# Seven-product groups combined in PSUM banks, and from group 1 on in the first FFN

## The chip, the cores and the metric

One core of a Trainium2 chip runs the whole program. Its engines work beside one another and each runs its own instructions in order: TensorE (PE; its weight loads are listed as PEld), VectorE (DVE), ScalarE (ACT), GpSimd (POOL) and SyncE (SP), which here does nothing but issue transfers. They meet at semaphores. The metric is the device time of one execution in microseconds; the median of three runs of the kernel before is 918.29 us.

## The reference

Two layers of an encoder over 256 tokens of width 1024, all float32. Each layer adds half of a SwiGLU FFN, then attention, then half of a second FFN; a last norm closes the trunk. The change concerns the four FFNs:

```python
def swiglu(h, w_gate, w_up, w_down):
    return (jax.nn.silu(h @ w_gate) * (h @ w_up)) @ w_down
...
    for l in range(DEPTH):
        x = x + 0.5 * swiglu(rms_norm(x, ffn1_norm[l]), ffn1_w_gate[l], ffn1_w_up[l], ffn1_w_down[l])
        ...
        x = x + 0.5 * swiglu(rms_norm(x, ffn2_norm[l]), ffn2_w_gate[l], ffn2_w_up[l], ffn2_w_down[l])
```

The gate and up matrices are 1024 x 2816, the down matrix is 2816 x 1024. The attention between them (windowed heads with a sink, and differential heads) is left as it is but for the PSUM banks that it uses.

## The kernel before

**Float32 by three products.** Every weight is split into a high part, which ScalarE casts, and a low part, which VectorE gets by subtracting it; activations are split alike. A product is three matmuls per chunk of 128 rows: high times high, low times high, high times low. Weights come as raw tiles of 512 rows by 512 columns (1 MB, six buffers, `N_RAW`), loaded by SP (line 153); each is split in two halves of 128x1024 into a pool of 28 tiles (`emit_split`, line 191).

**Order.** `specs` lists the weight steps in the order of use. `weights()` (line 249) takes the next one, and first lets `ahead()` (line 228) issue loads up to 10 steps ahead and splits up to `look` half steps ahead. So the place of every cast and subtraction in ScalarE's and VectorE's queues is fixed by where `weights()` is called and by `look`. All instructions are recorded by one helper (line 50), so the profile gives them the line L50; one has to go by tiles: `raw` is a loaded weight, `w` its parts, `s` activations and hidden values, `q` and `v` sums of activations, `ps` a bank, `tmp` an intermediate.

**One FFN.** The 2816 hidden columns are five groups of 512 (0 to 4) and a rest of 256. The down step of a group, two halves of 24 matmuls of 128x512, is interleaved with the products of the next group, so that TensorE has work while the hidden values are made and transposed.

**Seven products.** Gate and up of a group, for two token blocks and two halves of the 1024 rows, are eight products of 12 matmuls. `by_seven` (line 637) makes them with seven, in the manner of Strassen and Winograd, from sums of the activations (`make_sums`, line 349) and sums of the weights. With a the upper half of the gate matrix, b and c the upper and lower half of the up matrix and d the lower half of the gate matrix, the weights used are a, d, c, a+b, b+c, a+b+c and a+b+c+d. Two sums are made by accumulating DMAs on GpSimd's queue (`gather`, line 126: b into a, c into b), which read memory and add to the raw tile; two by VectorE in the raw tile (`plus`, line 131). `SEVEN` says which groups do so: 2 to 4 in the first FFN, 1 to 4 in the other three. Before, the step b+c stands near the front of the group, so that b is loaded early; the products go to separate banks, are copied out by ScalarE and combined by VectorE in five operations of 128x512.

**PSUM.** All eight banks belong to one rotating tag, `ps`.

**The start of the program.** The first FFN begins while its weights still arrive. GpSimd's queue there holds the norm's rsqrt (`r`), then the constants of the attention (small loads, an iota, a few small operations), then the first accumulating DMAs; these are held back by `issue` and let go by `flush` (lines 165 and 171).

Of the kernel before, what the change touches and what calls it, by code (L numbers as in the profile page):

```python
# [9 lines left out]
F32 = mybir.dt.float32  # L10
F32R = mybir.dt.float32r
AF = mybir.ActivationFunctionType
# [18 lines left out]
SEVEN = ((2, 3, 4), (1, 2, 3, 4))  # L31
# [3 lines left out]
def trunk(ctx: ExitStack, tc: tile.TileContext, x, n1, g1, u1, d1, nm, w_in, sink,  # L35
# [35 lines left out]
    def bank():  # L71
        return ps.tile([P, 512], F32, tag="ps", bufs=8, name=nm_("ps"))
# [19 lines left out]
    class Step:  # L92
        def __init__(self, kn, n, moves, key=None, prep=None, src=None, free=None, behind=None):
            self.kn, self.n, self.moves, self.prep = kn, n, moves, prep
# [20 lines left out]
    def seven(wg, wu, c0, downs, first):  # L115
# [112 lines left out]
    def ahead(n):  # L228

        n = min(n, 2 * len(specs) - 1)  # L230
        while True:
# [4 lines left out]
            elif at["prep"] <= min(n // 2 + 1, len(specs) - 1) and at["dma"] > at["prep"] and \  # L236
                    (specs[at["prep"]].prep is None or at["split"] >= 2 * at["prep"]):
# [21 lines left out]
    for l in range(DEPTH):  # L259
        def ffn_specs(wg, wu, wd, sevens):  # L260
# [45 lines left out]
    class Norm:  # L306
# [42 lines left out]
        def make_sums(self):  # L349
# [19 lines left out]
            s1 = add(b1, t1, ALU.subtract)  # L369
            s2 = add(s1, t0, ALU.add)  # L370
# [159 lines left out]
    def tokens(accs, xs, w, k0, ks=range(4), first=0, last=KC - 1, order=None, cols=slice(None), h=None):  # L530

        for k, t in (order or [(k, t) for k in ks for t in range(2)]):
            kk = k0 + k
            hi, lo = w.part(k, cols, h)
            xv = xs[kk // 2][:, kk % 2]
            xh, xl = xv[:, t * P:(t + 1) * P], xv[:, S + t * P:S + (t + 1) * P]
# [23 lines left out]
    def first_groups(norm, ws):  # L560

        sls = [halves(bank()) for _ in ws]
# [39 lines left out]
    def ffn(norm, aside=None, before=None, final=False, sevens=SEVEN[1]):  # L602
# [34 lines left out]
        def by_seven(h, g):  # L637
# [3 lines left out]

            def put(o, x, y, op):
                dve.tensor_tensor(o, x, y, op=op)
                return o

            late, run = g == max(sevens), 1 in sevens
            m1, m7 = flat(), flat()


            if g > 1:  # L650
                g0 = prod(norm.quarter(0, 0), weights())
                act.copy(m1, g0)
                p7 = prod(norm.summed(3), weights(1, True))
                act.copy(m7, p7)
                hT = turn(h, 2)
                prod(norm.quarter(0, 1), weights(), g0)
                p3 = prod(norm.summed(2), weights())
                if not run:
                    g0 = silu(flat(), g0, 0)
                down(hT, g - 1, 0, weights())  # L660
                if run:
                    g0 = silu(flat(), g0, 0)
            else:
                p1 = prod(norm.quarter(0, 0), weights(1, True))
                hT = turn(h, (0,))
                w = weights(1, True)
                act.copy(m1, p1)
                p2 = prod(norm.quarter(0, 1), w)
                hT += turn(h, (1,))
                g0 = put(flat(), p2, m1, ALU.add)  # L670
                down(hT, 0, 0, weights())
                silu(g0, g0, 0)
                p3 = prod(norm.summed(2), weights())
                p7 = prod(norm.summed(3), weights(1, True))
                act.copy(m7, p7)
            h = blk(F32)
            p5 = prod(norm.summed(0), weights())
            prod(norm.summed(1), weights(look[0] - 5 if late else run, late or run), p7)
            u1 = put(m1, p7, m1, ALU.subtract)
            p4 = prod(norm.quarter(1, 1), weights(look[0] - 4 if late else 3 * run, late or run))  # L680
            g1 = put(flat(), p4, u1, ALU.subtract)
            w = weights(look[0] - 3 if late else 2 * run)
            silu(g1, g1, 1)
            put(u1, u1, p5, ALU.subtract)
            u0 = put(m7, u1, m7, ALU.subtract)
            put(u0, u0, p3, ALU.add)
            if run and g == max(sevens) - 1:
                ahead(2 * at["use"] - 2 + look[0] - 1)
            up(h, u0, g0, 0)
            up(h, u1, g1, 1)  # L690
            down(hT, g - 1, 1, w)
# [14 lines left out]
        accs = [[bank(), bank()] for _ in range(2)]  # L706

        def down(hT, g, h, w):
# [453 lines left out]
```

## Time and profile before

| quantity | value |
| --- | --- |
| runs | 917.40, 918.29, 919.19 us; median 918.29 |
| profiled execution | 917.39 us, its span 915.6 us |
| granted TensorE clock, mean | 0.999 |
| 128x512 matmuls from weights | 2538 by `s`, 540 by `q`, 180 by `v` |
| weight splits of 128x1024 | 354 casts (ACT), 354 subtractions (DVE) |
| raw sums on VectorE, 128x1024 | 60 |
| accumulating DMAs (GpSimd's queue) | 30 of 1 MB |
| loaded by SP's queue, share of 16 DMA engines | 166.74 MB, 54.5% |
| accumulated, share of 16 DMA engines | 31.75 MB, 19.3% |

A group row of the profile names the operation with its tiles, the shapes, the count, then busy time and the mean of one in ns, then the idle time of the engine before it with what ended it. A timeline row gives start and duration in us, the engine, the operation and how many are merged; in brackets the idle time before and what ended it. A row of windows gives for a stretch of time how long each engine was busy, the granted TensorE clock, the share of the DMA engines and the rate. The time from issue to landing of a DMA counts from its instruction to the arrival of its data.

### The profile page before, as it was taken

What the parts mean: (1) busy time and instruction counts of PE and PEld (TensorE: products, weight loads), DVE (VectorE), ACT (ScalarE), POOL (GpSimd) and SP (SyncE); (2) the same over time, 40 slices, a digit from 0 to 9 for tenths busy, and PEclk for the clock granted to TensorE, in tenths of its full rate; (3) what the DMA queues carried; (4) which work ended last, traced back from release to release, by engine and by line L of the source; (5) the groups of instructions that cost most, each with busy time, mean ns of one, the idle gap of its engine ahead of it and who ended that gap; (6) DMA issues with size and microseconds to landing.
All of it is one profiled execution on the core that took longest, in us unless ns stands there. A gap on an engine that the chain in (4) does not pass through costs nothing.

```text
span 915.6 us, 12544 instructions
## 1 busy us (share of the span) xinstructions
PE 904.5 (99%) x4696; PEld 763.7 (83%) x4696; DVE 792.5 (87%) x1096; ACT 589.8 (64%) x917; POOL 66.4 (7%) x83
## 2 busy tenths in 40 slices
PE   8999999999999999999999999999999999999997
PEld 6888888899888888888888888888998888888886
DVE  6768999959975999999789999997797689999994
ACT  7836676557865766576486666665677496666561
POOL 0400100000010100100010010000001010010011
PEclk9999999999999999999999999999999999999999
DMA  9996898828436698898767998887463467998831
GB/s 339 355 238 173 265 297 268 238 93 240 136 108 189 158 280 248 257 273 275 258 164 201 276 285 217 265 293 219 116 230 98 139 153 201 275 289 230 259 132 47
DMA packets 114061, 200.87 MB, mean 219 GB/s; under 512 B 3662, under 2 KB 31376, under 8 KB 114000
## 3 DMA queue, kind: packets, MB, share of 16 engines
q1 hardware_dynamic: 96528, 166.74, 54.5%
q0 software_dynamic: 16096, 31.75, 19.3%
q10 hardware_dynamic: 1376, 1.57, 0.5%
q8 instruction: 37, 0.61, 0.3%
q14 instruction: 24, 0.20, 0.1%
HBM read 199.00 MB, written 1.05 MB: 218 GB/s over the span
## 4 chain that ended last, share of the span: by engine, by line
PE 98%; issue 1%; DMA 0%; ACT 0%; DVE 0%; POOLq 0%; POOL 0%; ACTq 0%
PE ps L50 98%; DMA xk<-in_x_dram 0%; ACT w L50 0%; DVE s L50 0%; DVE xk L50 0%; ACT tmp L50 0%; ACT L50 0%; POOLq L1157 0%; POOL rf L50 0%; ACTq L50 0%; DVE tot L50 0%; DVE tmp L50 0%
## 5 line engine op out<-in xcount | busy, mean ns | idle before, releaser
L50 PE MATMUL ps<-w,s 128*128 128x512 f32 (+1 forms) x2574 | 600.2, 391 | 0.5 <-ACT tmp L50 0.5
L50 PEld LDWEIGHTS ps<-w,s 128*128 128x128 f32 x2574 | 477.6, 188 | 100.3 <-ACT tmp L50 2.3
L50 DVE TENSOR_TENSOR w<-raw,w 128x1024 fp32r<-128x1024 f32 (+1 forms) x458 | 482.1, 1101 | 37.8 <-ACT w L50 36.6
L50 ACT CAST w<-raw 128x1024 fp32r<-128x1024 f32 (+1 forms) x458 | 409.8, 954 | 122.6 <-DVE raw L50 78.4
L50 PE MATMUL ps<-w,q 128*128 128x512 f32 x540 | 127.3, 389 | 0.0
L50 PEld LDWEIGHTS ps<-w,q 128*128 128x128 f32 x540 | 101.4, 188 | 21.0
L50 PE MATMUL ps<-s,w 128*128 128x256 f32 x672 | 83.1, 284 | 0.0
L50 PEld LDWEIGHTS ps<-s,w 128*128 128x128 f32 x672 | 81.5, 192 | 0.5
L50 POOL DMA_DIRECT2D raw<-in_ffn_w_up_dram x30 | 38.9, 1296 | 472.8 <-DVE w L50 240.8
L50 DVE TENSOR_TENSOR raw<-raw,raw 128x1024 f32<-128x1024 f32 x60 | 70.7, 1219 | 0.0
L50 ACT ACTIVATE s<-ps,gcol 128x256 fp32r<-128x256 f32 (+1 forms) x80 | 31.7, 480 | 43.7 <-PE ps L50 42.1
L50 ACT CAST s<-ps 128x512 fp32r<-128x512 f32 x44 | 24.3, 594 | 29.9 <-PE ps L50 29.9
L50 PE MATMUL ps<-w,v 128*128 128x512 f32 x180 | 43.3, 389 | 0.0
L50 ACT COPY tmp<-ps 128x512 f32<-128x512 f32 x34 | 19.9, 585 | 36.2 <-PE ps L50 34.0
L50 ACT ACTIVATE s<-s,negm 128x256 f32<-128x256 f32 x64 | 31.9, 500 | 14.8 <-DVE negm L50 14.8
L50 PE MATMUL ps<-ident,s 128*128 128x128 f32 x304 | 39.7, 273 | 0.0
L50 PEld LDWEIGHTS ps<-w,v 128*128 128x128 f32 x180 | 33.8, 188 | 7.0
L50 PEld LDWEIGHTS ps<-ident,s 128*128 128x128 f32 x304 | 35.1, 140 | 5.1 <-issue 0.8
L50 DVE TENSOR_TENSOR s<-ps,s 128x512 fp32r<-128x512 f32 x44 | 28.7, 686 | 9.1 <-ACT s L50 9.1
L50 DVE SCALAR_TENSOR_TENSOR s<-ps,gcol,s 128x256 fp32r<-128x256 f32 x48 | 20.3, 478 | 11.6 <-ACT s L50 11.5
L50 DVE TENSOR_TENSOR tmp<-ps,tmp 128x512 f32<-128x512 f32 x37 | 25.4, 686 | 2.7 <-PE ps L50 2.1
L50 DVE TENSOR_TENSOR xk<-xk,ps 128x512 f32<-128x512 f32 (+1 forms) x25 | 14.1, 598 | 14.9 <-PE ps L50 14.9
(106 smaller groups left out, 404.7 us busy)
## 6 DMA issues: line engine op xcount, KB each, us to landing
raw<-in_ffn_w_down_dram SPq DMA_DIRECT2D x44, 1024.0 KB, 8.9
raw<-in_ffn_w_gate_dram SPq DMA_DIRECT2D x39, 1024.0 KB, 6.4
raw<-in_ffn_w_up_dram SPq DMA_DIRECT2D x39, 1024.0 KB, 5.7
raw<-in_ffn_w_up_dram POOLq DMA_DIRECT2D x30, 1024.0 KB, 12.3
raw<-in_w_in_dram SPq DMA_DIRECT2D x14, 1024.0 KB, 6.1
raw<-in_ffn_w_gate_dram SPq DMA_DIRECT2D x8, 512.0 KB, 6.2
raw<-in_ffn_w_up_dram SPq DMA_DIRECT2D x8, 512.0 KB, 7.2
raw<-in_w_in_dram SPq DMA_DIRECT2D x8, 512.0 KB, 5.3
```

The source lines that it names most:

```text
L50: ins = issue(*a, **k)
```

## The change

All four FFNs make groups 1 to 4 with seven products. `by_sevens` holds all seven groups of an FFN in one function. ScalarE writes the negated first product into both halves of a two-bank tile (`xy`), and TensorE adds the products of two activation sums on top, one into each half. The product with a+b is copied by ScalarE into the bank of the first one before the product with a+b+c is added to it; the two activation sums involved change sign. VectorE combines the rest in three operations. The two-bank tile takes two of the eight banks and also serves other places: the up products of group 0, the rest, and some banks of the attention.

The second half of a group's down step moves into the next group, after its first product (`below`), and the hidden values are transposed by token (`turn_one`). The weight steps of a group become a, below, d, c, down, a+b, b+c, a+b+c, a+b+c+d, and b is loaded for the step b+c. In group 1 there is no `below` and the order is a, d, down, c. VectorE's sum of two raw tiles is one operation of 128x2048 instead of two of 128x1024, and is issued a step earlier (`early`). `lead` sets `look` per group.

```diff
-SEVEN = ((2, 3, 4), (1, 2, 3, 4))
+SEVEN = ((1, 2, 3, 4), (1, 2, 3, 4))
...
-        return ps.tile([P, 512], F32, tag="ps", bufs=8, name=nm_("ps"))
+        return ps.tile([P, 512], F32, tag="ps", bufs=6, name=nm_("ps"))
+
+    def pair():
+        return ps.tile([P, 2, 512], F32, tag="xy", bufs=1, name=nm_("xy"))
...
-    def seven(wg, wu, c0, downs, first):
+    def seven(wg, wu, c0, below, down):
...
-                for h in (0, 2):
-                    x_, t_ = [raws[i][:, h:h + 2] for i in (x, to)]
-                    dve.tensor_tensor(t_, t_, x_, op=ALU.add)
+                dve.tensor_tensor(raws[to], raws[to], raws[x], op=ALU.add)
             return prep
 
-        bc = Step(4, 512, load(b), key=b, behind=gather(c, b))
-        rest = [Step(4, 512, load(d), key=d, free=[]), Step(4, 512, load(c), key=c, free=[]), downs[0]]
-        steps = [rest[0], rest[2], rest[1], bc] if first else [bc] + rest
+        steps = [Step(4, 512, load(d), key=d, free=[]), Step(4, 512, load(c), key=c, free=[])]
+        steps = [below] + steps + [down] if below is not None else [steps[0], down, steps[1]]
         steps[0].prep = lambda: issue(gather(b, a), 1)
         return [Step(4, 512, load(a), key=a, free=[])] + steps + [
                 Step(4, 512, None, src=a, free=[]),
-                Step(4, 512, None, prep=plus(c, a), src=a, free=[c]),
-                Step(4, 512, None, prep=plus(d, a), src=a, free=[a, d]),
-                downs[1]]
+                Step(4, 512, load(b), key=b, behind=gather(c, b)),
+                Step(4, 512, None, prep=plus(c, a), src=a, free=[c], early=1),
+                Step(4, 512, None, prep=plus(d, a), src=a, free=[a, d])]
 
...
-                    (specs[at["prep"]].prep is None or at["split"] >= 2 * at["prep"]):
+                    (specs[at["prep"]].prep is None or at["split"] >= 2 * (at["prep"] - specs[at["prep"]].early)):
...
-                    specs.extend(seven(wg[l], wu[l], g * 512, downs, g == 1))
+                    specs.extend(seven(wg[l], wu[l], g * 512, down(g - 2, 1) if g > 1 else None, downs[0]))
+                    if g == max(sevens):
+                        specs.append(downs[1])
                 else:
                     specs.extend(plain(w[l], g * 512, 512, k0, 4) for w in (wg, wu) for k0 in (0, 4))
-                    specs.extend(downs)
+                    specs.extend(downs[:1] if g + 1 == min(sevens) else downs)
...
-            s1 = add(b1, t1, ALU.subtract)
-            s2 = add(s1, t0, ALU.add)
+            s1 = add(t1, b1, ALU.subtract)
+            s2 = add(t0, s1, ALU.subtract)
...
-        def by_seven(h, g):
...
+        def turn_one(h, t):
+            sl = bank()
+            for k in range(4):
+                pe.transpose(sl[:, k * P:(k + 1) * P], h[:, t, k * P:(k + 1) * P], ident)
+            hb = blk()
+            act.copy(hb[:, 0], sl)
+            dve.tensor_tensor(hb[:, 1], sl, f(hb[:, 0]), op=ALU.subtract)
+            return hb
+
+        def by_token(hb):
+            return lambda k, t: [hb[t][:, i, k * P:(k + 1) * P] for i in range(2)]
+
+        def by_chunk(hT):
+            return lambda k, t: [hT[k // 2][:, k % 2, i * S + t * P:i * S + (t + 1) * P] for i in range(2)]
+
+        def below(of, g, h, w, order=None):
+            while len(accs) <= h:
+                accs.append([bank(), bank()])
+            tokens(accs[h], of, w, 4 * g, last=(FC - 1, G4 - 1) if final and h else FC - 1, order=order)
+
+        def by_sevens(h, groups, old):
+            xy = pair()
+            for g in groups:
+                start, late = old is None, g == groups[-1]
+                look[0] = lead(g)
+                p1 = prod(norm.quarter(0, 0), weights(start, start))
+                act.activation(xy, p1.unsqueeze(1).to_broadcast([P, 2, 512]), AF.Copy, scale=-1.0)
+                if start:
+                    g0 = flat()
+                    act.copy(g0, p1)
+                new = [turn_one(h, 0)]
+                if start:
+                    p2 = prod(norm.quarter(0, 1), weights())
+                    new.append(turn_one(h, 1))
+                    dve.tensor_tensor(g0, p2, g0, op=ALU.add)
+                    below(by_token(new), g - 1, 0, weights(), [(k, t) for t in range(2) for k in range(4)])
+                    silu(g0, g0, 0)
+                    prod(norm.summed(2), weights(), xy[:, 1])
+                else:
+                    below(old, g - 2, 1, weights())
+                    new.append(turn_one(h, 1))
+                    prod(norm.quarter(0, 1), weights(), p1)
+                    prod(norm.summed(2), weights(), xy[:, 1])
+                    below(by_token(new), g - 1, 0, weights())
+                    g0 = silu(flat(), p1, 0)
+                old = by_token(new)
+                p5 = prod(norm.summed(0), weights())
+                act.copy(p1, p5)
+                prod(norm.summed(3), weights(), xy[:, 0])
+                prod(norm.summed(1), weights(look[0] - 5 if late else 1, True), p5)
+                e = flat()
+                act.copy(e, p5)
+                u1, u0 = flat(), flat()
+                dve.tensor_tensor(u0, xy[:, 1], e, op=ALU.add)
+                dve.tensor_tensor(u1, xy[:, 0], e, op=ALU.add)
+                h = blk(F32)
+                up(h, u0, g0, 0)
+                p4 = prod(norm.quarter(1, 1), weights(look[0] - 4 if late else 3, True), p1)
+                g1 = flat()
+                dve.tensor_tensor(g1, p4, u1, op=ALU.subtract)
+                if late:
+                    w = weights(look[0] - 3)
+                else:
+                    ahead(2 * at["use"] + look[0] - 2)
+                silu(g1, g1, 1)
+                up(h, u1, g1, 1)
+            below(old, groups[-1] - 1, 1, w)
...
-        accs = [[bank(), bank()] for _ in range(2)]
+        accs = []
+
+        def lead(n):
+            return IN_FFN - (n - min(sevens)) // 2 if before is not take_x else IN_MIX - (n == NGRP - 1)
 
         def down(hT, g, h, w):
+            while len(accs) <= h:
+                accs.append([bank(), bank()])
             tokens(accs[h], [None] * (2 * g) + hT, w, 4 * g, last=(FC - 1, G4 - 1) if final and h else FC - 1)
 
 
-        gs, us = [bank(), bank()], [bank(), bank()]
+        def both():
+            p = pair()
+            return [p[:, t] for t in range(2)]
+
+        gs, us = [bank(), bank()], both()
...
-                h = by_seven(h, n)
+                if n == min(sevens):
+                    h = by_sevens(h, sevens, by_chunk(hT) if n > 1 else None)
...
-        def scores(q, kb, dist, slopes, init, den):
-
-            sl = [bank(), bank()]
+        def scores(q, kb, dist, slopes, init, den, wide=False):
+
+            both = pair() if wide else None
+            sl = [both[:, i] if wide else bank() for i in range(2)]
```

More of the change, by code (lines that the diff above doesn't have):

```diff
@@ L92, in trunk, with __init__ @@
     class Step:
-        def __init__(self, kn, n, moves, key=None, prep=None, src=None, free=None, behind=None):
-            self.kn, self.n, self.moves, self.prep = kn, n, moves, prep
+        def __init__(self, kn, n, moves, key=None, prep=None, src=None, free=None, behind=None, early=0):
+            self.kn, self.n, self.moves, self.prep, self.early = kn, n, moves, prep, early
             self.behind = behind
@@ L560, in first_groups @@
     def first_groups(norm, ws):
-        sls = [halves(bank()) for _ in ws]
+        both = pair()
+        sls = [halves(both[:, i]) for i in range(2)]
         for k in range(0, KC, 2):
@@ L635, in prod @@
             return acc
-        def by_seven(h, g):
-            flat = lambda: tmp().rearrange("p a n -> p (a n)")
[L642 to L691, printed above, removed]
@@ L748, in ffn @@
             if n in sevens:
-                look[0] = IN_FFN + min(sevens) - n if before is not take_x else IN_MIX - (n == NGRP - 1)
-                h = by_seven(h, n)
+                if n == min(sevens):
+                    h = by_sevens(h, sevens, by_chunk(hT) if n > 1 else None)
                 continue
@@ L754, in ffn @@
             tokens(gs, norm.xs, weights(), 0)
+            norm.copies()
             hT = turn(h, 2)
-            norm.copies()
             next(sums, None)
@@ L760, in ffn @@
             next(sums, None)
-            us = [bank(), bank()]
+            us = both()
             for k0 in (0, 4):
@@ L765, in ffn @@
             h = hidden(g, us)
-            for hh in range(2):
+            for hh in range(1 if n + 1 == min(sevens) else 2):
                 down(hT, n - 1, hh, weights())
@@ L769, in ffn @@
                     next(sums, None)
-        gu = [bank(), bank()]
+        gu = both()
         tokens(gu, norm.xs, weights(), 0)
@@ L937, in mix @@
         vB = tp.tile([P, 2, 512], F32, tag="v", bufs=1, name=nm_("v"))
-        vsl = [bank() for _ in range(2)]
+        both = pair()
+        vsl = [both[:, t] for t in range(2)]
         for k0 in (0, 4):
@@ L984, in mix @@
         oT = [blk() for _ in range(4)]
-        rsl, osl = [[bank() for _ in range(2)] for _ in range(2)]
+        rsl, both = [bank() for _ in range(2)], pair()
+        osl = [both[:, t] for t in range(2)]
         for t in range(2):
```

9 lines of the change are left out of this document (6 added, 3 removed).

## The prediction

> **What bounds the kernel now.** I read the page's first part, the chain that ended last, TensorE's timeline, and then the other engines in the stretches that the change touches. The page's span and busy times:
>
> ```profile
> span 915.6 us, 12544 instructions
> ## 1 busy us (share of the span) xinstructions
> PE 904.5 (99%) x4696; PEld 763.7 (83%) x4696; DVE 792.5 (87%) x1096; ACT 589.8 (64%) x917; POOL 66.4 (7%) x83
> ```
>
> The chain of waits has one piece that is nearly the whole span:
>
> ```profile
> 31.04 873.94 PE ps L50 x4547
> ```
>
> TensorE runs without a gap from 31.04 to the end of the work, so a matmul saved is time saved, and anything that makes TensorE wait is time lost at full price. Its rate, from its timeline (start, duration, instructions):
>
> ```profile
> 6.47 6.87 PE L50 MATMUL ps<-w,s 128*128 128x512 f32 x24
> ...
> 31.04 5.76 PE L50 MATMUL ps<-w,s 128*128 128x512 f32 x24 [0.46 <-ACT tmp L50]
> 36.63 1.03 PE L50 MATMUL ps<-ident,s 128*128 128x128 f32 x8
> 37.42 30.18 PE L50 MATMUL ps<-w,s 128*128 128x512 f32 x132
> 67.44 2.89 PE L50 MATMUL ps<-w,v 128*128 128x512 f32 x12
> ```
>
> From 37.42 to 67.44 start 132 matmuls: 0.2274 us each, 2.73 for a product of 12, 5.46 for a down step of 24; eight transposes take 0.79 (36.63 to 37.42). A seven group is 7 x 2.73 + 2 x 5.46 + 0.79 = 30.8 us. Who is close behind? Busy times in the starting stretch and in one seven group of the second FFN:
>
> ```profile
> core 0: us, PE busy (x) PEld busy (x) DVE busy (x) ACT busy (x) POOL busy (x), PEclk, DMA share, GB/s
> 6.00:8.00 2.00, 2.00 (x8) 1.63 (x7) 1.80 (x4) 1.02 (x3) 0.00 (x0) 1.00 1.05 381
> 338.00:368.00 30.00, 30.00 (x138) 24.93 (x137) 29.68 (x30) 20.12 (x24) 2.57 (x2) 1.00 0.91 258
> ```
>
> VectorE 29.68 of 30 and the DMA engines at 0.91: the page's 87% hides that in these groups three resources are full at once. The change rearranges all three.
>
> **What is saved.** Group 1 of the first FFN takes seven products for eight: 12 matmuls, 2.73 us; the new bank order also has no wait like the 0.46 above. Per seven group VectorE loses two 128x512 combinations of five. Its rows in one group:
>
> ```profile
> 339.20 0.69 DVE L50 TENSOR_TENSOR tmp<-tmp,ps 128x512 f32<-128x512 f32 x1
> 339.92 1.42 DVE L50 SCALAR_TENSOR_TENSOR s<-tmp,hr,tmp 128x512 f32<-128x512 f32 x2
> 341.25 4.63 DVE L50 TENSOR_TENSOR w<-raw,w 128x1024 fp32r<-128x1024 f32 x4
> 345.79 1.29 DVE L50 TENSOR_TENSOR s<-ps,s 128x512 fp32r<-128x512 f32 x2
> ...
> 350.39 2.36 DVE L50 TENSOR_TENSOR raw<-raw,raw 128x1024 f32<-128x1024 f32 x2
> ```
>
> So a combination is 0.69, a hidden product 0.71, a weight's low part 1.16, a low part of h 0.64, a whole raw add 2.36 (I take the 128x2048 form as two halves; it cannot be much under). Two combinations fewer is 1.4 of 30 us; no gain by itself, as TensorE sets the group. ScalarE gains about 1.1 us a group (a copy of 128x1024 into the pair and a copy p1<-p5, for two copies of 0.585), inside its 10 idle us. Six banks and a pair for eight banks I take as free in the attention stage, where the pair comes back only two heads later; up to a few waits of 0.46 otherwise. ScalarE's prices:
>
> ```profile
> L50 ACT CAST w<-raw 128x1024 fp32r<-128x1024 f32 x354 | 352.3, 1053 | 120.5 <-DVE raw L50 78.4 <-DMA raw<-in_ffn_w_up_dram 40.3
> ...
> L50 ACT COPY tmp<-ps 128x512 f32<-128x512 f32 x34 | 19.9, 585 | 36.2 <-PE ps L50 34.0 <-DVE w L50 2.1
> L50 ACT ACTIVATE s<-ps,gcol 128x256 fp32r<-128x256 f32 x48 | 19.3, 474 | 43.7 <-PE ps L50 42.1 <-issue 1.6
> ...
> L50 ACT ACTIVATE tmp<-ps,r 128x512 f32<-128x512 f32 x22 | 14.6, 690 | 0.0
> ```
>
> **What is moved: the load of b (12 group changes).** A group loads a, below, d, c, down and now, last, b; with six raw buffers b's load takes the buffer that the group before frees last. By the semaphores of the built kernel it waits for the last VectorE split of that group's a+b+c+d. Call its end T. Before, b's load waited only for the split of b+c. After it, in GpSimd's queue, stand c-into-b, which needs b landed, and behind it b-into-a. Landings (us from issue, least/median/most), of two uncontended loads around 61 to 75, then of all 30 gathers:
>
> ```profile
> DMA to landing us min/median/max: 5.1/5.2/5.3
> ```
>
> ```profile
> DMA to landing us min/median/max: 8.4/12.3/15.0
> ```
>
> Two gathers behind one another: in the 8.6 us of the quickest, and in the stretch of the one issued at 301.71, the DMA views say
>
> ```profile
> q0 software_dynamic: 528, 1.05, 72.1%
> ```
>
> ```profile
> raw<-in_ffn_w_up_dram POOLq DMA_DIRECT2D x1, 1024.0 KB, 10.0
> ```
>
> One gather alone keeps all 16 engines busy for 0.721 x 8.6 = 6.2 us. So a pair lands 8.4 + 6.2 = 14.6 after the first issue at the least, 15.0 + 6.2 = 21.2 at the most. I take 15.0: few loads are then in flight. Then come ScalarE's cast (1.05) and VectorE's order: two splits of a+b, a low part of h, two of b+c, add, two of a+b+c, add, two of a+b+c+d: 8 x 1.16 + 0.64 + 2 x 2.36 = 14.6. From T to the next T: 5.2 + 15.0 + 1.05 + 14.6 = 35.9, against TensorE's 30.8: **5.1 per change**, 61 for the 12.
>
> Lower bound, no transfer late: the a+b+c product waits for the copy p1<-p5, which stands on ScalarE behind four casts and a SiLU (4 x 1.05 + 0.69 + 0.585 = 5.5 after the last raw add), and needs 5.46 with its successor; T is 2.3 after that add, so the group ends at T + 8.6. From that end VectorE has a combination, six splits, a hidden product and a low part (0.69 + 6.96 + 0.71 + 0.64 = 9.0), then the 14.6. 8.6 + 23.6 = 32.2, still 1.4 above 30.8. Upper: 5.2 + 21.2 + 1.05 + 14.6 = 42.1, 11.3 a change. Nothing here can gain: TensorE's 30.8 is the floor.
>
> [...]
>
> **Group 1 of the other three FFN stages.** VectorE's order puts four splits and a raw add (4 x 1.16 + 2.36 = 7.0) before the low part of h's second token, which the second half of the down step needs. TensorE before that group:
>
> ```profile
> 299.78 10.37 PE L50 MATMUL ps<-w,s 128*128 128x512 f32 x45
> 309.98 0.60 PE L50 MATMUL ps<-ident,s 128*128 128x128 f32 x4
> ```
>
> Its first product starts at 309.98 - 2.73 = 307.25; b-into-a lands at 301.71 + 10.0, that is 4.5 in. Cast, 7.0 and 0.64: 13.2. TensorE is there after 2.73 x 3 + 2 x 0.4 + 0.2 = 9.2. **Stall 4.0, three times 12**; 3.0 each at the least (landing 8.4), 6.3 with 12.3.
>
> **Group 1 of the first FFN.** GpSimd's queue is in order, and the gathers stand behind the constants:
>
> ```profile
> 26.79 0.72 POOL L50 TENSOR_TENSOR r<-ms,mhalf 128x2 f32<-128x2 f32 x1 [25.29 <-DVE ms L50]
> 27.45 0.75 POOL L50 DMA_DIRECT2D grow<-in_mix_norm_dram  x1
> ...
> 39.19 0.46 POOL L50 TENSOR_TENSOR s<-s 128x128 f32<-128x128 f32 x1 [1.52 <-DMA s<-in_lam_k_dram]
> 43.40 1.38 POOL L50 DMA_DIRECT2D raw<-in_ffn_w_up_dram  x1 [3.75 <-ACT w L50]
> ```
>
> ```profile
> 21.59 3.08 ACT L50 CAST w<-raw 128x1024 fp32r<-128x1024 f32 x3
> 24.57 0.63 ACT L50 ACTIVATE junk<-xk 128x512 f32<-128x512 f32 x1
> 25.10 0.19 ACT L50 ACTIVATION_READ_ACCUMULATOR junk<-xk 128x1 f32 x1
> 26.98 2.01 ACT L50 CAST w<-raw 128x1024 fp32r<-128x1024 f32 x2 [1.69 <-DMA raw<-in_ffn_w_up_dram]
> ```
>
> Now eight copies (0.474) and two casts stand ahead of the last squares: 24.6 + 3.8 + 2.1 + 0.7 = 31.2, and r comes 1.5 later, at 32.7 for 26.79. The constants end 5.9 later, at 45.6; b-into-a lands (10.0) at G = 55.6, c-into-b 6.2 later. From G: 6.2, a cast 1.05, split, add, split, two splits and add (4 x 1.16 + 4.72), two casts, copy: 19.1, at 74.7, when the a+b+c product may start. Unhindered it would at 30.58 + 2.73 x 5 + 5.46 + 0.8 = 50.5. **Stall 24**; 17 if the constants don't move and the gather takes 8.4, 29 with 15.0.
>
> **Sum.** 917.39 (the profiled execution; its span is 1.8 less) - 2.7 - 0.5 + 24 + 12 + 61 = 1011; the median of the runs is 0.9 above the profiled one: 1012.
>
> **Rivals.** (1) *Faster*: the queues hide all of it, 917.39 - 3.2 + 0.9 = 915. It needs a group's loop at 30.8: 1.4 less on VectorE and ScalarE together, and load plus pair in 30.8 - 15.7 = 15.1 where the least rows make 19.7. For it: VectorE was as full before and never late. 8%. (2) *Transfers are never late*, only the engines' orders: 917.39 - 3.2 + 17 + 9 + 12 x 1.4 + 0.9 = 958. For it: gathers no longer compete with as many loads; against it the 8.4. 20%. (3) *TensorE restarts slowly after each stall.* The first 24 matmuls at 6.47 took 6.87 for 24 x 0.2274 = 5.46, 1.4 more, though the granted clock there reads 1.00. After 16 stalls: 1012 + 22 = 1034. Against it: those matmuls may have waited for splits, and stalls come in pieces. 14%. [...] (4) *The pairs collide with loads*, 21.2: 12 x 11.3 for 61, 1087. 8%. That the matmuls aren't fewer is excluded by the built kernel's count (3246 for 3258 of 128x512).
>
> **Chances and range.** My forecast 48%, (2) 20, (3) 14, (4) 8, (1) 8, about no change 2. A measurement of this kernel tells 0.2% (1.8 us) from no change: faster 0.08, within 0.02, slower 0.90. The range 950 to 1050 takes in (2), (3) and half the way to (4), and leaves out (1) and most of (4).
>
> **What would show it.** The chain falls well below 98% TensorE, with the gathers, casts and VectorE's splits in it; TensorE's first stop is near 40 us, in the first FFN's group 1, and b-into-a is issued there at about 45. Within three groups of each FFN the issue of b's load follows the last split of a+b+c+d, the two gathers follow one another by under 2 us, their landings lie 13 to 17 after, and groups take 34 to 38. A granted clock under 1 would speak for (3). Wrong would be groups of 30.8, an unbroken TensorE, or landings under 10 us for both gathers.

## The result and the profile after

The changed kernel takes 1045.33 us (median of five runs, 1043.82 to 1047.52) against 918.29 before: a ratio of 1.138, 95% interval 1.136 to 1.140. The page of its profile, span and busy times, the granted clock in 40 slices, and the shares of the chain that ended last:

```profile
span 1042.0 us, 12435 instructions
## 1 busy us (share of the span) xinstructions
PE 947.5 (91%) x4684; PEld 783.3 (75%) x4684; DVE 786.4 (75%) x1048; ACT 610.9 (59%) x945; POOL 67.3 (6%) x85
...
PEclk9889889999999999998999999999999998998989
...
PE 39%; DMA 26%; DVE 20%; ACT 8%; issue 6%; POOL 1%; ACTq 0%; SPq 0%; POOLq 0%; DVEq 0%
```

Before, TensorE was 98% of that chain; now it is 39%, and DMA, VectorE and ScalarE make up 54%. TensorE is 43 us busier with 12 instructions fewer, and its granted clock now dips (0.954 in the mean, 0.999 before): both follow its waits, as will be seen. Its waits, summed (total, times, longest):

```profile
PE ps L50 <- ACT ps L50: 48.9, 13, 6.1
PE ps L50 <- DVE s L50: 22.7, 20, 5.0
PE ps L50 <- ACT s L50: 11.0, 6, 6.9
```

Where do the 127 us lie? GpSimd computes the rsqrt `r` once at each norm, so the starts of these rows in its timeline cut a run into stages. Differences from the kernel before, in us, from the profiled execution of this kernel and of all experiments below (the first column is from the span's start to the first attention's `r`; the last ends at the final norm):

| kernel | FFN 1 | attention 1 | FFN 2 | FFN 3 | attention 2 | FFN 4 |
| --- | --- | --- | --- | --- | --- | --- |
| before, us | 194.2 | 106.4 | 175.6 | 167.1 | 106.5 | 156.7 |
| the change | +38.1 | +0.5 | +28.7 | +28.7 | +0.5 | +29.3 |
| e1 first from group 2 | +15.0 | +0.5 | +28.5 | +26.9 | +0.5 | +28.4 |
| e2 gathers swapped | +19.5 | +0.6 | +10.9 | +9.1 | +0.5 | +9.3 |
| e3 b early | +36.4 | +0.5 | +21.5 | +25.5 | +0.5 | +23.5 |
| e4 warm | +37.9 | +0.5 | +30.3 | +29.7 | +0.6 | +28.6 |
| e6 copy first | +18.9 | +0.5 | +12.5 | +12.3 | +0.6 | +15.8 |
| e7 low part first | +20.3 | +0.5 | +9.0 | +11.3 | +0.5 | +12.6 |
| e8 gathers before constants | +11.9 | +0.5 | +8.9 | +11.2 | +0.5 | +12.9 |
| e9 first from group 2 | +2.4 | +0.5 | +10.8 | +11.1 | +0.5 | +12.9 |
| e10 b early, c late | +0.7 | +0.6 | +7.4 | +8.4 | +0.6 | +8.4 |
| e11 the same, all groups | +13.8 | +0.5 | +8.9 | +8.2 | +0.5 | +8.5 |
| e12 copy between | +0.4 | +0.6 | +5.8 | +6.5 | +0.5 | +5.8 |
| e13 the same, all groups | +17.1 | +0.5 | +6.7 | +6.4 | +0.5 | +5.6 |

The attention costs 0.5 each, so six banks and a pair are nearly free there; the loss is in the FFNs. In the second FFN, TensorE's timeline has the first of its two kinds of stall in group 1, then one stall in every group:

```profile
352.19 3.56 PE L50 MATMUL ps<-w,s 128*128 128x512 f32 x13
359.38 4.39 PE L50 MATMUL ps<-w,s 128*128 128x512 f32 x11 [3.64 <-DVE s L50]
...
374.49 5.60 PE L50 MATMUL ps<-w,s 128*128 128x512 f32 x24
...
408.00 4.54 PE L50 MATMUL ps<-w,q 128*128 128x512 f32 x12 [3.93 <-ACT ps L50]
412.37 5.62 PE L50 MATMUL ps<-w,s 128*128 128x512 f32 x24
```

At 359.38 the down step's second half waits for the low part of the second token's h, which VectorE makes after four splits and a raw sum. At 408.00 the a+b+c product waits for ScalarE's copy p1<-p5. The rows at 374.49 and 412.37 each hold a group's a+b+c+d product and the next group's first; from one to the other a group takes 37.9 us for the 30.8 that TensorE needs (36.1 to 41.5 over the whole run). What sets it is read from the other queues. SP's issue of b's load, and GpSimd's issue of the two gathers:

```profile
406.47 0.37 SPq L153 DMA_DIRECT2D raw<-in_ffn_w_up_dram  x1
...
444.58 0.37 SPq L153 DMA_DIRECT2D raw<-in_ffn_w_up_dram  x1
```

```profile
373.77 2.59 POOL L50 DMA_DIRECT2D raw<-in_ffn_w_up_dram  x2 [32.09 <-DVE w L50]
412.23 2.59 POOL L50 DMA_DIRECT2D raw<-in_ffn_w_up_dram  x2 [35.87 <-DMA raw<-in_ffn_w_up_dram]
```

Both come every 38.1 to 38.5 us here, and in groups 2 to 4 the two gathers always come as a pair without a gap. Between them stands this, on ScalarE and then on VectorE:

```profile
427.43 1.05 ACT L50 CAST w<-raw 128x1024 fp32r<-128x1024 f32 x1 [6.42 <-DMA raw<-in_ffn_w_up_dram]
```

```profile
428.51 1.23 DVE L50 TENSOR_TENSOR w<-raw,w 128x1024 fp32r<-128x1024 f32 x1 [4.45 <-ACT w L50]
...
441.81 1.23 DVE L50 TENSOR_TENSOR w<-raw,w 128x1024 fp32r<-128x1024 f32 x1 [1.19 <-ACT w L50]
443.33 4.77 DVE L50 TENSOR_TENSOR w<-raw,w 128x1024 fp32r<-128x1024 f32 x4 [0.30 <-ACT w L50]
```

So one turn is: b's load (406.47 to the pair's issue, 5.8), the pair (412.23 to 427.43, 15.2), and 17.1 of ScalarE and VectorE until the last split of a+b+c+d frees the buffer for the next b at 444.58: 38.1. Over the eight whole turns of the run it is 37.3 to 39.2, in the mean 38.4: 5.5 to 5.8 for the load, 14.8 to 17.1 for the pair, 16.3 to 17.2 for ScalarE and VectorE.

Group 1 of the first FFN stops in other places. TensorE, and ScalarE with the cast that waits for b-into-a:

```profile
38.52 1.11 PE L50 MATMUL ps<-ident,s 128*128 128x128 f32 x4 [5.01 <-DVE s L50]
...
53.91 0.80 PE L50 MATMUL ps<-w,s 128*128 128x512 f32 x1 [6.89 <-ACT s L50]
...
69.37 3.04 PE L50 MATMUL ps<-w,q 128*128 128x512 f32 x12 [1.00 <-ACT ps L50]
```

```profile
51.39 1.99 ACT L50 CAST w<-raw 128x1024 fp32r<-128x1024 f32 x2 [10.18 <-DMA raw<-in_ffn_w_up_dram]
```

### The profile page after: what moved, and what is told of

It is laid out like the page before. It is cut to its first block, busy times and chain, and to the rows that moved or that the text cites. A ratio compares the mean times of both kernels' runs of the same rounds, so it can differ in the third digit from the quotient of the medians.

```text
span 1042.0 us, 12435 instructions
## 1 busy us (share of the span) xinstructions
PE 947.5 (91%) x4684; PEld 783.3 (75%) x4684; DVE 786.4 (75%) x1048; ACT 610.9 (59%) x945; POOL 67.3 (6%) x85
## 3 DMA queue, kind: packets, MB, share of 16 engines
q0 software_dynamic: 17152, 33.84, 18.6%
HBM read 201.10 MB, written 1.05 MB: 194 GB/s over the span
## 4 chain that ended last, share of the span: by engine, by line
PE 39%; DMA 26%; DVE 20%; ACT 8%; issue 6%; POOL 1%; ACTq 0%; SPq 0%; POOLq 0%; DVEq 0%
PE ps L50 28%; DMA raw<-in_ffn_w_up_dram 23%; DVE w L50 11%; PE xy L50 11%; DVE raw L50 7%; ACT w L50 4%; ACT s L50 2%; DVE s L50 2%; DMA raw<-in_ffn_w_gate_dram 1%; DMA xk<-in_x_dram 1%; DMA s<-in_lam_k_dram 1%; ACT tmp L50 1%; DVE tmp L50 0%; POOL raw L50 0%; ACT xy L50 0%
## 5 line engine op out<-in xcount | busy, mean ns | idle before, releaser
L50 PE MATMUL ps<-w,s 128*128 128x512 f32 (+1 forms) x2034 | 495.4, 398 | 26.4 <-DVE s L50 16.0
L50 PEld LDWEIGHTS ps<-w,s 128*128 128x128 f32 x2034 | 383.0, 192 | 113.2 <-DVE s L50 20.0
L50 PE MATMUL xy<-w,s 128*128 128x512 f32 x480 | 114.2, 391 | 0.0
L50 PEld LDWEIGHTS xy<-w,s 128*128 128x128 f32 x480 | 89.4, 188 | 18.4
L50 DVE TENSOR_TENSOR raw<-raw,raw 128x2048 f32<-128x2048 f32 x32 | 73.2, 2289 | 0.5
L50 PE MATMUL ps<-s,w 128*128 128x256 f32 x480 | 59.3, 284 | 0.0
L50 PEld LDWEIGHTS ps<-ident,s 128*128 128x128 f32 x304 | 35.4, 141 | 17.2 <-DVE s L50 10.5
L50 PE MATMUL xy<-w,v 128*128 128x512 f32 x192 | 46.4, 390 | 1.1 <-DVE w L50 1.1
L50 PE MATMUL xy<-w,q 128*128 128x512 f32 x192 | 47.0, 394 | 0.0
L50 DVE TENSOR_TENSOR tmp<-xy,tmp 128x512 f32<-128x512 f32 x32 | 20.6, 686 | 32.9 <-ACT tmp L50 32.9
L50 PEld LDWEIGHTS xy<-w,q 128*128 128x128 f32 x192 | 37.1, 193 | 8.0
L50 PEld LDWEIGHTS xy<-w,v 128*128 128x128 f32 x192 | 36.0, 188 | 8.9 <-DVE w L50 1.5
## 6 DMA issues: line engine op xcount, KB each, us to landing
raw<-in_ffn_w_up_dram POOLq DMA_DIRECT2D x32, 1024.0 KB, 11.3
```

The source lines that it names most:

```text
L50: ins = issue(*a, **k)
```

## The experiments

My theory is the loop of load, pair and VectorE's chain, and for the first FFN the gathers behind the constants; the rivals are TensorE's slow restarts and full engines. Each run is an edit of the changed kernel or, where one is named, of an earlier run; e10 puts several edits together. e1 to e4, e6 and e7 were timed once each, the others four or five times, with a spread of at most 0.4%.

**e1: the first FFN from group 2 on.**

```diff
-SEVEN = ((1, 2, 3, 4), (1, 2, 3, 4))
+SEVEN = ((2, 3, 4), (1, 2, 3, 4))
```

> One edit to the changed kernel: the first FFN makes seven products only from group 2 on, as before. My theory (the first FFN's group 1 waits for gathers that stand behind the constants on GpSimd, 19 us by the trace of the changed kernel, and one group change more at 7 to 11): the time falls by 19 + 8 - 2.7, to about 1021 us, and TensorE has no wait of several us before 75 us. Rival (the start costs what it costs whatever group begins, the wait only moves to group 2): above 1035.

Measured 1017.81 us (before beside it 917.88). The table shows that only the first FFN moves, by 23.1: with the 2.7 of the matmuls given back, group 1 there and its group change cost 26. As expected, TensorE has no wait of several us before 75 us; the first is 6.13 at 122.22.

**e2: the gathers swapped.** c-into-b is kept back until b-into-a of the same group is issued.

```diff
+        def second(add):
+            def go():
+                if turn_["ba"]:
+                    add()
+                else:
+                    turn_["cb"] = add
+            return go
+        def first_():
+            issue(gather(b, a), 1)
+            turn_["ba"] = True
+            if turn_["cb"] is not None:
+                issue(turn_["cb"], 2)
...
-        steps[0].prep = lambda: issue(gather(b, a), 1)
+        steps[0].prep = first_
...
-                Step(4, 512, load(b), key=b, behind=gather(c, b)),
+                Step(4, 512, load(b), key=b, behind=second(gather(c, b))),
```

> One edit to the changed kernel: on GpSimd's queue b-into-a is issued before c-into-b; loads, buffers and every other order stay. My theory (the loop load of b, pair of gathers, VectorE's chain sets the group's period of about 38): b-into-a no longer waits for b's load, the first splits after it run while c-into-b is under way, and the period falls by 3 to 5 in 11 or 12 changes: 985 to 1010 us. Rival (the chain on VectorE and ScalarE or TensorE's slow restarts set the period): over 1035.

Measured 967.68 us: 78 us for one order of two instructions on a queue whose engine is 7% busy. GpSimd's timeline in the second FFN:

```profile
386.73 1.29 POOL L50 DMA_DIRECT2D raw<-in_ffn_w_up_dram  x1 [30.91 <-DVE w L50]
391.10 1.28 POOL L50 DMA_DIRECT2D raw<-in_ffn_w_up_dram  x1 [3.08 <-DMA raw<-in_ffn_w_up_dram]
420.82 1.31 POOL L50 DMA_DIRECT2D raw<-in_ffn_w_up_dram  x1 [28.43 <-DVE w L50]
```

b-into-a now goes out as soon as a is split, while b is still loading. TensorE's groups, from one a+b+c+d product to the next:

```profile
388.37 5.61 PE L50 MATMUL ps<-w,s 128*128 128x512 f32 x24
...
420.98 5.61 PE L50 MATMUL ps<-w,s 128*128 128x512 f32 x24
...
453.40 6.96 PE L50 MATMUL ps<-w,s 128*128 128x512 f32 x30
```

32.6 and 32.4; over the run 31.7 to 32.9, in the mean 32.2, which is what the prediction gives for engines whose transfers are never late. The theory's range began at 985; the time fell further than that, since the period fell by 6 us a change and not by 3 to 5.

**e3: b early.** The step b+c and its product stand behind the below step, so that b's load takes a buffer that comes free early.

```diff
-        steps = [below] + steps + [down] if below is not None else [steps[0], down, steps[1]]
+        bc = Step(4, 512, load(b), key=b, behind=gather(c, b))
+        steps = [below, bc] + steps + [down] if below is not None else [steps[0], down, steps[1], bc]
...
-                Step(4, 512, load(b), key=b, behind=gather(c, b)),
-                Step(4, 512, None, prep=plus(c, a), src=a, free=[c], early=1),
+                Step(4, 512, None, prep=plus(c, a), src=a, free=[c]),
```

The product moves along with its step. The edit also takes back `early`, so VectorE's first raw sum is issued a step later.

> One edit to the changed kernel: the step b+c and its product move to the front of a group (after the below step; in group 1 after c), so that b is loaded early into a buffer that comes free early, as in the kernel before. My theory (b's load behind the last split of a+b+c+d opens the loop): the gathers part, groups fall from about 38 to 32 or 33, the time by 12 x 5 to about 985 us; what is left over the kernel before is the first FFN's group 1 and the stalls of the other groups 1. Rival (the DMA engines have no room for both gathers in a group): over 1030.

Measured 1025.49 us: a miss. The loads and gathers do what was meant (the gathers are issued 10 to 12 us apart), but a group still takes 34.2 to 37.8:

```profile
399.71 2.88 PE L50 MATMUL ps<-w,q 128*128 128x512 f32 x12
405.79 4.61 PE L50 MATMUL ps<-w,q 128*128 128x512 f32 x12 [3.20 <-ACT ps L50]
```

```profile
430.79 2.36 DVE L50 TENSOR_TENSOR w<-raw,w 128x1024 fp32r<-128x1024 f32 x2 [1.12 <-ACT w L50]
433.19 2.29 DVE L50 TENSOR_TENSOR raw<-raw,raw 128x2048 f32<-128x2048 f32 x1
436.67 5.77 DVE L50 TENSOR_TENSOR w<-raw,w 128x1024 fp32r<-128x1024 f32 x5 [1.19 <-ACT w L50]
```

The product with b+c no longer lies between the one with a+b and the one with a+b+c, so nothing covers the copy between them; and its splits no longer lie behind the first raw sum, so VectorE idles for ScalarE's cast after both sums. One wait went and two others took its place. How much of the second comes from the missing `early` isn't shown.

**e4: TensorE kept busy through the wait.**

```diff
+                w1 = weights(look[0] - 5 if late else 1, True)
+                for _ in range(16):
+                    pe.matmul(xy[:, 0], lhsT=zero, rhs=norm.xs[0][:, 0], start=False, stop=False, skip_group_check=True)
-                prod(norm.summed(1), weights(look[0] - 5 if late else 1, True), p5)
+                prod(norm.summed(1), w1, p5)
```

> One edit to the changed kernel: 16 matmuls with a zero operand (3.64 us), added into the pair where they change nothing, stand before each a+b+c product, so that TensorE works through most of the wait there. Theory A (the low granted clock after each wait, 4.4 to 5.5 us for 12 matmuls that take 2.73, is paid at every group change): the product takes 2.7 to 3.0 again and the time falls by 12 x 2 or more, to 1021 us or less. Theory B (the loop of load, gathers and VectorE sets the period, and the slow product lies beside it): the product is quick again but the time falls only where no further group follows, 4 x 2, to about 1037 us. If the clock isn't the cause, the product stays at 4.4 or more and the time rises or stays.

Measured 1045.46 us, against 1045.33 without: no change. TensorE's timeline in the second FFN and GpSimd's in the first:

```profile
407.74 3.79 PE L50 MATMUL xy<-s,zero 128*128 128x512 f32 x16
411.37 2.88 PE L50 MATMUL ps<-w,q 128*128 128x512 f32 x12
```

```profile
75.59 2.59 POOL L50 DMA_DIRECT2D raw<-in_ffn_w_up_dram  x2 [30.44 <-DVE tmp L50]
113.81 2.59 POOL L50 DMA_DIRECT2D raw<-in_ffn_w_up_dram  x2 [35.63 <-DMA raw<-in_ffn_w_up_dram]
```

The product at 411.37 takes 2.88 instead of 4.5 to 5.5. In the changed kernel the granted clock is 0.64 over the one of 4.54 at 408.00, and 1.00 over one of 2.88 at 398.46, so the clock is what slowed it. The gathers still come every 37 to 40 us (38.2 in these rows), so the slow product lay beside the loop. Theory B has the mechanism, but its 8 us were not seen: the last group of each FFN didn't get shorter, but 0.3 to 2.6 us longer. In the second FFN TensorE now waits 2.54 for h at 470.69, just after the pair's landing at 469.03, and the 20 matmuls after that take 7.57 for 4.55. The zero matmuls themselves add 3.6 to each group 1 of the last three FFNs, where there is no such wait, and the loop takes in a part of it.

**e6: the copy ahead of the last splits** (on top of e2).

```diff
-                p5 = prod(norm.summed(0), weights())
+                p5 = prod(norm.summed(0), weights(look[0] - 5, True))
...
-                    below(by_token(new), g - 1, 0, weights())
+                    below(by_token(new), g - 1, 0, weights(max(0, look[0] - 7), True))
```

In group 1 the product with c, which stands before the one with a+b there, gets the same edit as the down step.

> Two edits to the changed kernel: the gathers swapped as in the run before, and the splits of a+b+c+d queued behind ScalarE's copy p1<-p5 instead of ahead of it. My theory (with the gathers swapped, groups of 32.5 are set by VectorE's chain and the copy behind the casts): groups fall to TensorE's 30.8 and the time by 12 x 1.6 from 967.7 to about 948 us; the waits for ScalarE's copy, 9.6 us in 10 places, go. Rival (VectorE is simply full at 32.5): 965 or more.

Measured 978.38 us, 11 more than e2: a miss. TensorE's waits for the copy are gone, but those for VectorE's `s` rise from 18.2 to 34.1 us: ScalarE now stands still until p5 is done, with the casts queued behind the copy. e9, which has the same edit, shows it, ScalarE first, then VectorE:

```profile
365.81 0.57 ACT L50 COPY ps<-ps 128x512 f32<-128x512 f32 x1 [4.71 <-PE ps L50]
```

```profile
367.37 6.90 DVE L50 TENSOR_TENSOR w<-raw,w 128x1024 fp32r<-128x1024 f32 x6 [3.09 <-ACT w L50]
```

**e7: the low part of h first** (on top of e6).

```diff
-                    p2 = prod(norm.quarter(0, 1), weights())
+                    p2 = prod(norm.quarter(0, 1), weights(look[0] - 5, True))
```

> One edit more: in group 1 of every FFN the splits of a+b and b+c are queued behind the high and low part of h's second token instead of ahead of them. My theory: the stall of 3.6 us and its slow restart, together 5.9, go in three FFNs: 18 less, about 930 us; the first FFN's group 1 stays late, since its a+b+c product hangs on the gathers. Rival (the same work only comes later, and stalls the a+b product): 942 or more.

Measured 972.04 us: 6.3 less than e6, where 18 were expected. In the table the second to fourth FFN gain 3.5, 1.0 and 3.2; the rival is nearer, the late splits come later instead. Group 1 of the second FFN now runs without a stop, but from its a+b+c+d product to group 2's it takes 36.5 us where e6 has 33.4.

**e8: the gathers before the constants** (on top of e7).

```diff
-            constants()
-            flush()
+            flush()
+            constants()
```

> One edit more: at the start GpSimd issues the two gathers of the first FFN's group 1 before the attention's constants. My theory: b-into-a lands some 11 us earlier, c-into-b is held by b's landing at about 42 and lands at about 53, so the first group's stall falls from 19 to about 8: 11 less than the run before, about 920 us. Rival (the stall comes from b's late load, not from the constants): no more than 4 less.

Measured 963.79 us (ratio to before 1.049, 1.047 to 1.050): 8.3 less than e7, all of it in the first FFN: between the theory's 11 and the rival's 4, nearer the theory. So the place behind the constants was 8 of the late start's cost. b-into-a goes out with `r`, and c-into-b with it, not held for b as expected:

```profile
30.74 1.02 POOL L50 TENSOR_TENSOR r<-ms,mhalf 128x2 f32<-128x2 f32 x1 [29.24 <-DVE ms L50]
31.71 2.81 POOL L50 DMA_DIRECT2D raw<-in_ffn_w_up_dram  x2
```

**e9: as e7, with e1's line `SEVEN = ((2, 3, 4), (1, 2, 3, 4))`, so the first FFN from group 2 on.**

> The three repairs of the order (gathers swapped, copy first, low part first) with seven products only from group 2 on in the first FFN, as in the kernel before: the 12 matmuls are given back, and with them the late start. My theory: nothing stalls, TensorE's chain is unbroken, the time is that of the kernel before or a little under, 916 to 919 us. Rival (six banks and the pair, or VectorE, still cost a few us per FFN): 925 or more.

Measured 955.22 us (ratio 1.039, 1.037 to 1.041): the theory missed, the rival holds. The first FFN is nearly free at +2.4; the others keep 11 to 13 each. In the second FFN 7 of its 11 lie between group 1's a+b+c+d product and group 2's, where TensorE waits 2.25 and 2.53 us for VectorE's h; after the second wait and four transposes, 12 matmuls take 4.58 us for 2.73 at 350.22. I put them down to the copy's order (above) and to c-into-b, which still needs the late b; how much belongs to which isn't shown here.

**e10: b early, c late** (on top of e9).

```diff
-        steps = [below] + steps + [down] if below is not None else [steps[0], down, steps[1]]
+        bc = Step(4, 512, load(b), key=b, behind=gather(c, b) if below is not None else second(gather(c, b)))
+        steps = [below, bc, steps[0], down] if below is not None else [steps[0], down, steps[1]]
+        cs = Step(4, 512, load(c), key=c, free=[])
...
-                Step(4, 512, load(b), key=b, behind=second(gather(c, b))),
+                bc if below is None else cs,
...
+                i_ = 3 if start else 2
-                prod(norm.summed(3), weights(), xy[:, 0])
+                prod(norm.summed(i_), weights(), xy[:, 3 - i_])
```

Beside it the second raw sum is made in two halves, c-into-b stands on GpSimd's queue behind b's early load, and c itself is loaded in b's old place.

> The run with the first FFN from group 2 on and the three repairs, with one more change of order: b's load and the product with b+c move to the front of a group, c's product moves between the one with a+b and the one with a+b+c, c-into-b is issued as soon as b has landed, and the second raw sum of VectorE is made in two halves, so that no cast waits for the whole. My theory (with both gathers behind the last split, load and pair still make 32.5 of every group; VectorE needs 30.0 a group and loses 1.1 at each sum that nothing covers): groups fall to about 31, TensorE's waits to under 10 us, the time to 916 to 926 us. Rival (VectorE and ScalarE in this order cannot make a group under 32): 945 or more.

Measured 944.06 us (ratio 1.028, 1.027 to 1.030): better, and between the two expectations, nearer the rival's 945. Groups 3 and 4 of the last three FFNs still take 32.3, and group 2 takes 35.3 to 36.9: the copy's place costs VectorE 2 to 3 us in each, as in e9.

**e11: e10 with all groups (`SEVEN` as in the change), and the gathers before the constants (e8's edit).**

> The same with seven products from group 1 on in the first FFN, as in the change, and the two gathers of its group 1 ahead of the constants. It has the 12 matmuls fewer (2.7 us) and the late start, 8 to 11 us by the pair of runs before. My theory: 5 to 9 us above the run beside it. Rival (the late start is absorbed where the groups have slack): below the run beside it.

Measured 957.21 us, 13.2 above e10 where 5 to 9 were expected: 13.1 of it in the first FFN.

**e12: the copy between** (on top of e10): behind the casts of a+b+c+d, ahead of those of the next group.

```diff
-                p5 = prod(norm.summed(0), weights(look[0] - 5, True))
+                p5 = prod(norm.summed(0), weights(max(0, look[0] - 7), True))
...
-                    below(by_token(new), g - 1, 0, weights(max(0, look[0] - 7), True))
+                    below(by_token(new), g - 1, 0, weights())
```

> The run with b early and c late from group 2 on in the first FFN, with one edit taken back in part: ScalarE's copy p1<-p5 now stands behind the two casts of a+b+c+d but ahead of those of the next group. My theory (in the run before, ScalarE waits 3.5 to 4.5 us a group for p5 with the casts queued behind it, VectorE then 2 to 3 us for them, and the hidden values come late): VectorE's gaps before a+b+c+d go, groups fall from 32.3 to 31, the time from 944 to between 917 and 928 us. Rival (VectorE cannot make a group of 30.0 busy us in 31 whatever the order): 938 or more.

Measured 936.96 us (ratio 1.020, 1.019 to 1.022). The groups are near what was forecast: 31.3 from one a+b+c+d product to the next in these rows, 30.9 to 32.9 over the run, with VectorE's gap for ScalarE's cast at 0.30 us:

```profile
366.58 5.61 PE L50 MATMUL ps<-w,s 128*128 128x512 f32 x24
...
397.91 5.61 PE L50 MATMUL ps<-w,s 128*128 128x512 f32 x24
```

```profile
392.35 1.23 DVE L50 TENSOR_TENSOR w<-raw,w 128x1024 fp32r<-128x1024 f32 x1
393.88 1.23 DVE L50 TENSOR_TENSOR w<-raw,w 128x1024 fp32r<-128x1024 f32 x1 [0.30 <-ACT w L50]
```

The time is not, and lies near the rival's 938: about 6 us stay in each of the second to fourth FFN, most of it at their start:

```profile
330.83 3.02 PE L50 MATMUL ps<-w,q 128*128 128x512 f32 x12 [2.46 <-ACT ps L50]
...
347.01 0.66 PE L50 MATMUL ps<-ident,s 128*128 128x128 f32 x4 [1.81 <-DVE s L50]
```

These two rows are group 1's a+b+c product and group 2's transposes. Which edit would remove them was not tried.

**e13: e12 with all groups and the gathers before the constants, as in e11.**

> The same with group 1 of the first FFN by seven products too, and its gathers ahead of the constants: the best version that I have of what the change means to do. My theory: the late start of the first group costs 8 to 13 us, the 12 matmuls give 2.7: 6 to 12 above the run beside it. Rival (with shorter groups the start is caught up): equal to the run beside it or below.

Measured 951.61 us (ratio 1.037, 1.036 to 1.038), 14.7 above e12 where 6 to 12 were expected. With seven products in group 1, the first FFN costs 17 us even with its gathers early (in the profiled execution, which is 2.8 us above the median); one row of it is group 2's transposes at 81.68, which wait 7.48 us for VectorE.

No version beats the kernel before; e12 is the best of the new form, 19 us behind. Not tried: a seventh raw buffer.

## Why the prediction was right, step by step

The forecast was 1012 us, the measured time is 1045: 33 us more, and 5 us under the upper end of a range that reached so far only to take in rival (3) and half the way to (4). The mechanism was right; the terms of the group changes and of the later groups 1 were too small.

- **TensorE bounds, so stalls cost their full length**: right for the kernel before. In the changed kernel TensorE is 39% of the chain, and in e4 the 3.6 us of matmuls added before every a+b+c product left the time as it was, because the loop sets the period.
- **The loop through b's late load** (5.1 a change, 61): right in mechanism, too small in size. One turn was predicted as 5.2 + 15.0 + 1.05 + 14.6 = 35.9 and measured as 38.4 in the mean, 5.7 + 15.9 + 16.9. The term that was mis-sized most is the last, ScalarE's cast and VectorE's chain, 16.9 for 15.65: in the turn shown VectorE idles 1.19 and 0.30 for ScalarE's casts behind the second raw sum, which I counted as if the casts ran ahead. The pair adds 0.9, load and hand-over to GpSimd 0.5. TensorE's groups 2 to 4 took 92 us more than 12 x 30.8, that is 7.7 a change: 31 of the 33 us. e2 shows the loop itself: with nothing changed but the two gathers' order, 78 us go.
- **The lower bound of a group by engines alone, 32.2**: e2's are 32.2 in the mean.
- **Group 1 of FFNs 2 to 4** (4.0 each): the wait is 3.64, but the 11 matmuls after it take 4.39 for 2.50. In all 345.91 to 377.21 (the second half of the row at 374.49) is 31.3 for 25.4 of work: 5.9, of which 1.9 is the slow restart. All three come to 18.6 for the 12 forecast. The least that the prediction gives, 3.0 with a landing of 8.4, is by its own rows 2.4, so the 9 in rival (2) would be 7.
- **Group 1 of the first FFN** (24): its first product starts at 30.62, and group 2's at 74.97, for 25.4 of work: 19. The a+b+c product started at 69.37 and not at 74.7, mainly because `r` came at 30.75, not 32.7, and the constants ended 3 us earlier than worked out: b-into-a landed at 51.36 for 55.6, and the chain behind it took 18.0 for 19.1 (whose terms add up to 19.3). The place was not as forecast: that product itself waits only 1.00. TensorE had stopped before, 6.89 at 53.91 for a cast of h that stands on ScalarE behind the cast for b-into-a, and 5.01 at 38.52 (hidden values late with `r`), which I had in no term; as I read it, the gathers set the start of the a+b+c product, so this stop adds nothing. e8 shows 8 us as the constants' part. Of the 7 that stay in e8's group 1, the first stop (4.04 at 38.50) and the slow restart after it (5.33 for 2.73) make 6.6.
- **Six banks and the pair free in the attention**: 0.5 each.
- **Rival (2), transfers never late**: e2 is about that case, 967.7 for the 958 worked out. Its twelve changes cost 17.1, for 12 x 1.4 = 16.8; the rest is in the groups 1.
- **Rival (3), slow restarts**: its 1034 is nearer to the measured time than my 1012, but by luck: the 22 us that it adds are not where the missing 33 lie. The restarts exist, contrary to the 1.00 of the starting rows: in the changed kernel, products of 12 matmuls take 4.5 to 5.5 us after waits of 2.97 to 6.13, at a granted clock of 0.50 to 0.65, and the clock row dips to 0.8; after a wait of 1.00 one takes 3.04 at 1.00. But e4 takes most of them away in the group changes and the time stays (1045.46 for 1045.33). In group 1, where TensorE is the late one, they are paid. The length of the wait alone doesn't foretell them: over the runs a wait of 2.46 was enough in one place, and one of 3.65 was not in another (last section).

## What to carry to other kernels

A queue whose engine is nearly idle (6% busy in the changed kernel) can still set the time: two instructions of 1.3 us in the wrong order on GpSimd were 78 us here, because one that was ready stood behind one that waited. When buffers rotate, ask which earlier instruction frees the buffer of each load, and follow load, transfer and splits back to that instruction: if the turn is longer than the bound engine's period, it is the new period (here 38.4 us for 30.8). And where an engine makes a sum that another must cast before it can go on, count the cast's length as idle time unless other work lies between (in the turn shown, ScalarE's casts take 1.05 and VectorE idles 1.19 for one).

## What the runs showed of the hardware

A pair of accumulating 1 MB transfers, issued one behind the other, landed 13.7 to 17.5 us after the first issue in the changed kernel, and one alone took 8.4 at the least in the kernel before. After a wait of 6.13 us the granted clock was 0.50 over the product at 108.48 in the changed kernel, and 0.50 also after one of 2.97 at 145.80, but the length of the wait alone doesn't decide it. In the timelines of the changed kernel, e2, e3 and e4, products of 12 matmuls took 3.01 to 3.06 us after waits of 0.50 to 2.36 us directly before them, and 4.54 to 5.49 after waits of 3.88 to 6.13; between 2.46 and 3.65 both occur. These two rows of e3 show the same wait before 3.06 and before 4.61 us (in the changed kernel a product of 3.04 at 69.37 has a granted clock of 1.00, one of 4.61 at 444.78 has 0.63):

```profile
111.10 3.06 PE L50 MATMUL ps<-w,q 128*128 128x512 f32 x12 [3.65 <-ACT ps L50]
...
146.39 4.61 PE L50 MATMUL ps<-w,q 128*128 128x512 f32 x12 [3.65 <-ACT ps L50]
```

A wait of 2.46 was followed by 3.02 us for 12 matmuls in e12 at 330.83, and by 4.61 in e4 at 146.18.
